# A two-layer hybrid trunk on one core: second MLP operand by quarters, stored products loaded at another product, decays loaded ahead of step sizes

## The chip, the cores and the metric

The kernel runs on one core of a Trainium2 chip. The time is the device time of one execution in microseconds; 2805.24 us is the median of three runs (2802.8 to 2806.19). In the profile, PE is TensorE's matmuls, PEld its weight loads, DVE is VectorE, ACT is ScalarE, POOL is GpSimd and SP is SyncE. POOL and SP mostly issue DMAs here: SP the weights and the mixers' small transfers, POOL most of the activations'.

## The reference, cut to what matters

The input is 1024 prompt tokens and 8 sample tokens of width 1024. Each of two layers is a token mixer and an MLP, both between a modulated norm and a gated residual:

```python
h = rmsnorm(x, norm_mix[l]) * (1.0 + s1) + sh1
out, S, buf = even_mixer(h, ...) if l % 2 == 0 else mamba_mixer(h, ...)
x = x + g1 * out
h = rmsnorm(x, norm_mlp[l]) * (1.0 + s2) + sh2
x = x + g2 * (jnp.square(jax.nn.relu(h @ mlp_w1[l])) @ mlp_w2[l])
```

`mlp_w1` is 1024 x 4096 and `mlp_w2` 4096 x 1024. The odd mixer is a chunked state-space recurrence: a step size `dt` per token and head, its running sum, and the decay `exp` of differences of that sum within a chunk; the sample tokens take one recurrent step of their own. All is float32.

## The kernel before

**Stages.** In the profiled span of 2804.9 us the even mixer takes the first 537 us, its MLP runs to about 1274, the odd mixer to about 2107, the second MLP to the end.

**Precision.** Each float32 operand is split in a high and a low part (ACT copies the high part, DVE subtracts it), and each product is three matmuls, on lines 490 (high x high), 493 and 494. Their operands in a row are `whi`, `wlo` (weights) and `rr`, `hh`, `hl`, `hr`, `x` (activations); `pd` is the accumulator in PSUM.

**The MLP.** Each of its two matrix products is cut 2 x 2, and seven products of sums of the blocks stand for eight. The first half (`AOPS`, loop at line 865) runs over 16 pairs `p` of output rows, with products `q` from 1 to 7. For the pairs in `SPLIT` (the first two and the last four, 12 to 15, among them) products 1 and 2 are done well ahead of the others, and their results go to DRAM: product 1 as `kept` (line 895), the squared ReLU of product 2 as `b` (line 806). They come back when the pair's other products run: `kept(p)` (line 856) loads product 1 into a buffer `t`, and line 886 loads `b` into a slot of `x`. Pair 12 calls for them at its product 6, whose result L899 subtracts from the loaded one. That subtraction is also what frees the product's accumulator, so a later matmul waits for it. POOL issues all of these DMAs, strictly in the order of the code, and a store waits at its head until ACT or DVE has made its data. Ahead of pair 12's product 6 in that queue stand the stores of pair 15's products 1 and 2 and the four loads that `load_op(0, 0)` issues at the end of (15, 2).

**The second half** (loop at line 939) makes products `i` = 0 to 6, each in eight steps `j` of 48 matmuls (the last product in 16 half steps). From `i` = 1 on, steps 0 to 3 take the quarters `q` = 0 to 3 of the operand for one half of the outputs, steps 4 to 7 again for the other. Operand `i` lies in DRAM (`td`) and comes by `load_op(i, kh)` for its halves `kh` = 0 and 1: two tiles `rr`, one for the high parts and one for the low; four loads of two rows of blocks each, issued on POOL; and four chunks of a split, ACT's copy on L843 and DVE's subtraction on L844, that `split_op` hands out at the ends of steps by a table of counts (lines 974 to 977). I call the chunks of the second half chunk 0 to 3: step 2 reads chunks 0 and 1, step 3 chunks 2 and 3. For `i` from 2 to 5 chunk 0 is split at the end of step 7 of the product before, chunks 1 and 2 at the end of step 0, chunk 3 at the end of step 1. A tile's buffers are those of the product before, so loads for a half are issued at step 5 (`kh` = 1 of the next product) and step 7 (`kh` = 0 of the one after).

Between those steps DVE also builds the weights: L451, L453 and L455 add or subtract two weight blocks that SP's loads bring (`t<-W`, `t<-sd`, `raw<-W`), ACT makes the high part on L456, DVE the low part on L457. DVE runs its queue in order, so a chunk of `rr` behind such a sum waits for that sum's DMA too. L964 and L971 apply a finished accumulator to `x`. In the first MLP, steps also hold work on the next layer's modulation (`t<-ada`, L320).

**The odd mixer** works in two halves of the tokens. `odd_dt` makes step sizes, stores the running sums (`csd`), their exponentials (`esd`) and the last column (`cdd`), and for the first half the sample tokens' step sizes (`sd`). A background generator, `rest()`, is stepped along with the other work: it loads `dts` (from `sd`) and `cd`, then transposes on PE. Later `odd_ssd` loads, for each chunk, two broadcast blocks of `csd` (`load(r)`), on which ACT works on L1533. SP's order in this stage is set by a scheduler as it builds the program, not by the code's order alone.

Of the kernel before, what the change touches and what calls it, by code (L numbers as in the profile page):

```python
# [8 lines left out]
F32R = mybir.dt.float32r  # L9
# [5 lines left out]
P = 128  # L15
D = 1024
KT = 8
# [144 lines left out]
def kernel(ctx: ExitStack, tc: tile.TileContext, A: dict):  # L162
# [62 lines left out]
    def dma_aux(out, in_):  # L225

        tc.keep_in_program_order(nc.gpsimd.dma_start(out=out, in_=in_))  # L227
# [557 lines left out]
    def mlp(l, gi, finish, more=None):  # L785
# [44 lines left out]

        R, todo = {}, []

        def load_op(i, kh):

            pool, tag = ((big, M["tags"][0]), (ph.pool, "hr"), (big, M["tags"][1]))[BSET[i][kh]]
            ts = [pool.tile([P, KT * 520], F32R, name="rr", tag=tag, bufs=2) for _ in range(2)]
            hi, lo = R[i, kh] = [t[:, 0:KT * HX].rearrange("p (k t) -> p k t", t=HX) for t in ts]
            d = td[BOPND[BPROD[i]]][kh]

            def parts():  # L840
                for c in range(0, KT, 2):
                    src = lo[:, c:c + 2].bitcast(F32)
                    tc.keep_in_program_order(S.copy(hi[:, c:c + 2], src))  # L843
                    V.tensor_sub(lo[:, c:c + 2], src, hi[:, c:c + 2].bitcast(F32))  # L844
                    yield
            for c in range(0, KT, 2):
                dma_aux(lo[:, c:c + 2].bitcast(F32), d[:, c:c + 2])
            todo.append(parts())

# [15 lines left out]
        for i, (p, q) in enumerate(AOPS):  # L865
            n = APOS[p, q]
            while len(got) <= n // 2:
                got.append(need(f"a{l}", len(got), AHEAD - 1))
            if i == 0:
                bg.drain(hgen.pop(3, None))  # L870
                sg = bg.add(mlp_sums())
                bg.step(sg)
            elif i == 2 * LEAD:
                bg.drain(hgen.pop(2), sg)
                sg = bg.add(mlp_more_sums())
            elif i == 2 * LEAD + 4:
                bg.drain(sg)
            if i == 2 * LEAD - 4:
                kept(0)
                kept(1)  # L880
            if q == 6:
                kept(p)
                if p and p + 1 in keep:
                    kept(p + 1)
            if p in SPLIT and q == (5 if p < 2 else 6):
                dma_aux(slot(p, 1), B[p])
            w = 512 * (n % 2), got[n // 2]
            pt = pd()
            product(w, q, pt)
            pv = pt[:, :, 0:HX // 2]  # L890
            if q == 1:
                U[p, 1] = t2(HX)
                S.copy(v2(U[p, 1]), pv)
                if p in SPLIT:
                    keep[p] = dr.tile([P, HX], F32, name="kept", tag=f"kept{p}")
                    dma_aux(keep[p], U[p, 1])
            elif q == 6:
                U[p, 1], U[p, 2] = saved.pop(p, U[p, 1]), t2(HX)
                V.tensor_sub(v2(U[p, 2]), v2(U[p, 1]), pv)  # L899
            elif q == 7:  # L900
                U[p, 3] = t2(HX)
                V.tensor_add(v2(U[p, 3]), pv, v2(U[p, 2]))
            elif q == 5:
                c = t2(HX)
                V.tensor_add(v2(c), pv, v2(U[p, 3]))
                V.tensor_add(v2(U[p, 2]), pv, v2(U[p, 2]))
                ff_out(p, q, c, -1.0)
            elif q == 2:
                c = t2(HX) if p in SPLIT else U[p, 1]
                V.tensor_add(v2(c), pv, v2(U[p, 1]))  # L910
                ff_out(p, q, c, 1.0)
            elif q == 4:
                c = U[p, 3] if p < NPAIR - 1 else t2(HX)
                V.tensor_add(v2(c), pv, v2(U[p, 3]))
                ff_out(p, q, c, -1.0)
            else:
                V.tensor_add(v2(U[p, 2]), pv, v2(U[p, 2]))
                ff_out(p, q, U[p, 2], 1.0)
            if n % 2:
                prepare(wpos[0] - 1 + AHEAD)  # L920
            if (p, q) == FRONT[1][-1]:
                load_op(0, 0)
            elif p == NPAIR - 2 and q in (7, 5, 4, 3):
                split_op()
            if (p, q) == (NPAIR - 1, 5):
                split_op(4)
                load_op(0, 1)
            bg.tick(2)

        x = new_x()  # L930
        for m in range(KT):
            dma_aux(x[:, m, :], xd[:, m])
        load_op(1, 0)
        acc = tp.tile([P, KT, NS], F32, name="racc", tag="racc", bufs=2)
        V.memset(acc, 0.0)
        fin = finish()
# [2 lines left out]
        for n, (i, hb, q, mp) in enumerate(BOPS):  # L939
            j = n % 8  # L940
            hi, lo = need(f"b{l}", n, AHEAD - 1)
            if n == 8 and more:
                ada[0] = more()
            elif i == 6 and hb == 0 and j == 0:
                ada_steps(99)
            rh, rl = R[i, q // 2]
            seq = BSEQ if i else BFIRST
            qs = [qq for qq, mm in seq if mm == mp]
            for m in (2 * mp, 2 * mp + 1):
                if q == qs[0]:  # L950
                    pts[m] = pd()
                pt = pts[m]
                for b in range(2) if hb is None else (hb,):
                    c = slice(b * hw, b * hw + hw)
                    mm3(pt[:, b, 0:hw], [(hi[:, o:o + P], lo[:, o:o + P], rh[:, k, c], rl[:, k, c])
                                         for k, o in ((q % 2 * 4 + k, 256 * k + m % 2 * P) for k in range(4))],
                        q == qs[0], q == qs[-1])
                if q == qs[-1]:
                    for o, th in BOUT[BPROD[i]]:
                        mt = 4 * o + m  # L960
                        gate = mod[:, gi + mt, 0:1]
                        if hb is None:
                            xv = v2(x[:, mt, th * HX:th * HX + HX])
                            V.scalar_tensor_tensor(xv, pt[:, :, 0:hw], gate, xv, op0=ALU.mult, op1=ALU.add)  # L964
                        else:
                            xv = x[:, mt, th * HX + hb * hw:th * HX + hb * hw + hw]
                            V.scalar_tensor_tensor(xv, pt[:, hb, 0:hw], gate, xv, op0=ALU.mult, op1=ALU.add)
                        if hb != 1:
                            sv = pt[:, 0, 0:4] if th else pt[:, 1, hw - 4:hw]
                            av = acc[:, mt, 4 * th:4 * th + 4]  # L970
                            V.tensor_add(av, sv, av)  # L971
            prepare(wpos[0] - 1 + AHEAD)

            if i == 0:
                split_op((0, 2, 2, 0, 1, 1, 2, 0)[j])
            else:
                split_op((2, 2, 1, 1, 1, 1, 0, 1)[j] if i == 1 else (2, 1, 1, 1, 1, 1, 0, 1)[j] if i < 6 else (2, 1, 0, 0, 0, 0, 0, 0)[j] if hb == 0 else 0)
            if j == (5 if i else 3) and i < 6:
                load_op(i + 1, 1)
            elif j == 7 and i < 5:  # L980
                load_op(i + 2, 0)
# [372 lines left out]
    def dtile(w=136):  # L1354
        t = ph.pool.tile([P, 136], F32, name="dtr", tag="dtr", bufs=4)
        return t[:, :w]

    def odd_dt(hf, o):

        u = need("dt", 0)  # L1360
# [53 lines left out]
            o.dts = ph.pool.tile([P, 2, 16, NS], F32, name="dts")  # L1414

        def rest():
            yield
            if hf == 0:
                for q in range(2):
# [4 lines left out]
            yield  # L1424
            pt = psm()
            PE.transpose(pt[:, 0:P], dtt[:, 0:P], ident)
            PE.transpose(pt[:, P:2 * P], cs[:, 0:P], ident)
            PE.transpose(pt[:, 2 * P:3 * P], dl, ident)
            o.nat = hs3[:, 0:3]
            V.tensor_copy(o.nat.rearrange("p a t -> p (a t)"), pt[:, 0:3 * P])  # L1430
        return bg.add(rest())

    def odd_conv(hf, t, unit, dst):
# [46 lines left out]
    def odd_ssd(hf, g, o):  # L1480
# [6 lines left out]
        St = o.S[g]  # L1487

        def load(r):
            hs = 32 * r + 8 * g  # L1490
            Rs = []
            for q in range(2):
                R = t2(512)
                dma(R, o.csd[hs + 4 * q:hs + 4 * q + 4].rearrange("(o h) t -> o (h t)", o=1).broadcast_to([P, 512]))
                Rs.append(R)
            return Rs

        def load_e(r):
            hs = 32 * r + 8 * g
# [17 lines left out]
            PE.matmul(pc[:, c], Bt[:, c], Ct[:, c], start=True, stop=True)  # L1517
        cb = t3(512)
        V.tensor_mul(a4(cb), a4(pc), cmask.unsqueeze(1).broadcast_to([P, 4, P]))
        Rs = load(0)  # L1520
        yield
        for r in range(4):
            c = slice(r * P, r * P + P)
# [604 lines left out]
```

## Time and profile before

| What | us |
|---|---|
| median of three runs | 2805.24 |
| profiled execution | 2806.7 |
| its span | 2804.9 |
| PE busy | 2654.7 |
| DVE busy | 1983.5 |
| ACT busy | 1485.0 |
| mean granted clock | 0.977 of full speed |

A row of the timeline names the start, the duration, engine, line, operation, output and inputs, and in brackets the idle time ahead of it with what ended that. A row of the waits gives the total, the number of waits and the longest. A row of the windows gives, for one stretch, its length, each engine's busy time with its number of instructions (PE, PEld, DVE, ACT, POOL), the granted clock, the mean busy share of the 16 DMA engines and GB/s.

### The profile page before, as it was taken

The numbers are of one execution on the slowest core, as the hardware profiler recorded it, in microseconds if no ns is written. First come the engines' busy times: TensorE is split into PE (matmuls) and PEld (weight loads), VectorE is DVE, ScalarE is ACT, GpSimd is POOL, SyncE is SP. The second block draws the span as 40 slices with busy tenths as digits, with TensorE's granted clock in tenths as the row PEclk, the third lists the DMA queues.
The fourth block names the chain that finished last, engine by engine and source line by source line (L and its number), as shares of the span: only waits on it lengthen the run. The fifth ranks groups of instructions, "written<-read, shape, count | busy, mean of one in ns | idle before, by whom it ended". The sixth has DMA issues, their size and how long they took to land. (4 is left out here: it accounts for less than half of the span.)

```text
span 2804.9 us, 49250 instructions
## 1 busy us (share of the span) xinstructions
PE 2654.7 (95%) x19442; PEld 2443.9 (87%) x19442; DVE 1983.5 (71%) x3668; ACT 1485.0 (53%) x2409; POOL 266.5 (10%) x492
## 2 busy tenths in 40 slices
PE   6999999999999988998899999999999999999897
PEld 4889888899999977898789897787779999999897
DVE  5666544788757555775789788998778776756676
ACT  5785511464444322356687767878756445433234
POOL 0000000023223100000000000000001322311000
PEclk9999999999999999999899999999999999999998
DMA  8232333257468899834545745444435655779764
GB/s 300 69 107 71 105 121 113 88 191 242 168 204 312 328 334 353 321 129 115 142 148 144 184 122 155 132 132 124 117 105 172 223 184 181 264 284 372 266 214 156
DMA packets 199256, 525.63 MB, mean 187 GB/s; under 512 B 32688, under 2 KB 50736, under 8 KB 199024
## 3 DMA queue, kind: packets, MB, share of 16 engines
q1 hardware_dynamic: 150640, 355.25, 40.3%
q0 software_dynamic: 48384, 167.23, 16.2%
q8 instruction: 153, 2.51, 0.4%
q14 instruction: 79, 0.65, 0.1%
HBM read 408.59 MB, written 113.80 MB: 186 GB/s over the span
## 5 line engine op out<-in xcount | busy, mean ns | idle before, releaser
L490 PE MATMUL pg<-hh,whi 128*128 128x256 f32 (+2 forms) x1616 | 535.8, 332 | 13.5 <-ACT hh L592 6.2
L493 PE MATMUL pd<-rr,whi 128*128 128x258 f32 x1792 | 512.3, 286 | 25.1 <-DVE rr L844 24.9
L493 PE MATMUL pg<-hl,whi 128*128 128x256 f32 (+2 forms) x1616 | 522.8, 324 | 1.9 <-DVE hl L593 1.9
L494 PE MATMUL pg<-hh,wlo 128*128 128x256 f32 (+2 forms) x1616 | 522.0, 323 | 0.0
L490 PE MATMUL pd<-rr,whi 128*128 128x258 f32 x1792 | 513.4, 287 | 0.0
L494 PE MATMUL pd<-rr,wlo 128*128 128x258 f32 x1792 | 510.5, 285 | 1.5 <-DVE wlo L467 1.1
L467 DVE TENSOR_TENSOR wlo<-raw,whi 128x1024 fp32r<-128x1024 f32 x222 | 270.7, 1221 | 216.5 <-ACT whi L466 209.9
L466 ACT CAST whi<-raw 128x1024 fp32r<-128x1024 f32 x222 | 231.4, 1044 | 349.4 <-PE pg L493 192.0
L493 PEld LDWEIGHTS pd<-rr,whi 128*128 128x128 f32 x1792 | 343.6, 192 | 29.2 <-DVE rr L844 27.0
L490 PEld LDWEIGHTS pd<-rr,whi 128*128 128x128 f32 x1792 | 343.7, 192 | 19.0 <-issue 16.5
L490 PEld LDWEIGHTS pg<-hh,whi 128*128 128x128 f32 x1616 | 308.0, 191 | 50.0 <-issue 8.8
L494 PEld LDWEIGHTS pd<-rr,wlo 128*128 128x128 f32 x1792 | 344.0, 192 | 4.0 <-DVE wlo L467 1.8
L493 PEld LDWEIGHTS pg<-hl,whi 128*128 128x128 f32 x1616 | 308.1, 191 | 31.1 <-issue 5.8
L494 PEld LDWEIGHTS pg<-hh,wlo 128*128 128x128 f32 x1616 | 307.4, 190 | 24.4 <-issue 0.7
L490 PE MATMUL pd<-hh,whi 128*128 128x258 f32 x1024 | 293.9, 287 | 18.6 <-DVE t L899 12.6
L493 PE MATMUL pd<-hh,whi 128*128 128x258 f32 x1024 | 292.7, 286 | 0.8 <-DVE hh L695 0.8
L494 PE MATMUL pd<-hh,wlo 128*128 128x258 f32 x1024 | 291.1, 284 | 0.0
L490 PEld LDWEIGHTS pd<-hh,whi 128*128 128x128 f32 x1024 | 196.8, 192 | 21.0 <-issue 13.6
L456 ACT CAST whi<-t 128x1024 fp32r<-128x1024 f32 x64 | 67.0, 1047 | 274.8 <-PE pd L493 116.8
L493 PEld LDWEIGHTS pd<-hh,whi 128*128 128x128 f32 x1024 | 196.3, 192 | 1.9 <-DVE hh L695 1.4
L494 PEld LDWEIGHTS pd<-hh,wlo 128*128 128x128 f32 x1024 | 196.6, 192 | 0.0
L490 PE MATMUL pg<-ffh,whi 128*128 128x264 f32 (+2 forms) x544 | 176.8, 325 | 2.1 <-ACT bcz L1633 1.5
(335 smaller groups left out, 5813.9 us busy)
## 6 DMA issues: line engine op xcount, KB each, us to landing
raw<-W SPq DMA_DIRECT2D x375, 512.0 KB, 4.3
td<-x POOLq DMA_DIRECT2D x224, 258.0 KB, 3.6
rr<-td POOLq DMA_DIRECT2D x112, 516.0 KB, 8.1
t<-ada SPq DMA_DIRECT2D x192, 256.0 KB, 5.4
t<-W SPq DMA_DIRECT2D x32, 512.0 KB, 5.8
sd<-t SPq DMA_DIRECT2D x32, 512.0 KB, 5.8
t<-sd SPq DMA_DIRECT2D x32, 512.0 KB, 5.5
t<-csd SPq DMA_DIRECT2D x64, 256.0 KB, 4.6
```

The costliest lines, as they stand in the source:

```text
L456: S.copy(hi, h)
L466: S.copy(hi, raw)
L467: V.tensor_sub(lo, raw, hi.bitcast(F32))
L490: mm = PE.matmul(pt, wh, xh, start=first and i == 0, stop=False)
L493: PE.matmul(pt, wh, xl, start=False, stop=False)
L494: PE.matmul(pt, wl, xh, start=False, stop=last and i == n - 1)
```

## The change

It has three parts.

1. The second half's operands are loaded by quarters: `load_op(i, q)` makes one tile per quarter that holds high and low parts, with two loads and two chunks of a split. The same loads and chunks are issued as before, the quarters 2 and 0 at step 4 and 6 (of product 0: 2 and 6), the quarters 3 and 1 at step 5 and 7 (3 and 7). The split's tables change: for `i` from 2 to 5 chunks 0 and 1 are split at the end of step 7, chunk 2 at the end of step 0 and chunk 3 at the end of step 1.
2. The loads of `kept` for pairs 12 and 13 and of `b` for pair 12 move from (12, 6) to (15, 1), where they are issued ahead of that product.
3. In the odd mixer, `rest()` first loads the two blocks of `csd` for the first chunk of group 0 (`o.R0`), then makes the transposes, then loads `dts` and `cd`. `odd_ssd` takes them from there for its first chunk.

```diff
-        def load_op(i, kh):
+        def load_op(i, q):
...
-            pool, tag = ((big, M["tags"][0]), (ph.pool, "hr"), (big, M["tags"][1]))[BSET[i][kh]]
-            ts = [pool.tile([P, KT * 520], F32R, name="rr", tag=tag, bufs=2) for _ in range(2)]
-            hi, lo = R[i, kh] = [t[:, 0:KT * HX].rearrange("p (k t) -> p k t", t=HX) for t in ts]
-            d = td[BOPND[BPROD[i]]][kh]
+            pool, tag = ((big, M["tags"][0]), (ph.pool, "hr"), (big, M["tags"][1]))[BSET[i][q // 2]]
+            t = pool.tile([P, KT * 520], F32R, name="rr", tag=tag, bufs=2)
+            hi, lo = R[i, q] = [t[:, j * 4 * HX:(j + 1) * 4 * HX].rearrange("p (k t) -> p k t", t=HX)
+                                for j in range(2)]
+            d = td[BOPND[BPROD[i]]][q // 2][:, q % 2 * 4:q % 2 * 4 + 4]
...
-            if p in SPLIT and q == (5 if p < 2 else 6):
+            if p in SPLIT and q == (5 if p < 2 else 6) and p != NPAIR - TAIL:
                 dma_aux(slot(p, 1), B[p])
+            elif (p, q) == (NPAIR - 1, 1):
+                kept(NPAIR - TAIL)
+                kept(NPAIR - TAIL + 1)
+                dma_aux(slot(NPAIR - TAIL, 1), B[NPAIR - TAIL])
...
-            if i == 0:
-                split_op((0, 2, 2, 0, 1, 1, 2, 0)[j])
-            else:
-                split_op((2, 2, 1, 1, 1, 1, 0, 1)[j] if i == 1 else (2, 1, 1, 1, 1, 1, 0, 1)[j] if i < 6 else (2, 1, 0, 0, 0, 0, 0, 0)[j] if hb == 0 else 0)
-            if j == (5 if i else 3) and i < 6:
-                load_op(i + 1, 1)
-            elif j == 7 and i < 5:
-                load_op(i + 2, 0)
+            split_op(((0, 2, 1, 1, 1, 1, 1, 1), (2, 2, 1, 1, 1, 1, 0, 2), (1, 1, 0, 0, 0, 0, 0, 0))[2 if i == 6 else i][j]
+                     if i in (0, 1, 6) else (1, 1, 1, 1, 1, 1, 0, 2)[j])
+            at = (4, 5, 6, 7) if i else (2, 3, 6, 7)
+            if j in at and i < 6 and i + 1 + at.index(j) // 2 < 7:
+                load_op(i + 1 + at.index(j) // 2, (2, 3, 0, 1)[at.index(j)])
...
         def rest():
+            o.R0 = load_decays(o, 0)
+            yield
...
-        Rs = load(0)
+        Rs = load(0) if g else o.R0
```

What this does to the order of instructions is seen at three places. The first is POOL's queue at the end of the first MLP's first half; `kept<-t` and `b<-t` are the stores of pairs 13 to 15, `t<-kept` the loads for pairs 12 and 13, `x<-b` that of pair 12. Before:

```order
L227 DMA b_8178<-t_8174 128x516
L227 DMA kept<-t_8220 128x516
L227 DMA b_8253<-t_8249 128x516
L227 DMA kept<-t_8286 128x516
L227 DMA b_8319<-t_8315 128x516
L227 DMA rr<-td 128x1032 x4
L227 DMA t_8341<-kept 128x516 x2
L227 DMA x<-b_8112 128x516
```

And now:

```order
L227 DMA b_8178<-t_8174 128x516
L227 DMA kept<-t_8220 128x516
L227 DMA b_8253<-t_8249 128x516
L227 DMA t_8261<-kept 128x516 x2
L227 DMA x<-b_8112 128x516
L227 DMA kept<-t_8290 128x516
L227 DMA b_8323<-t_8319 128x516
L227 DMA rr<-td 128x1032 x4
```

The three loads stand ahead of pair 15's two stores and of the four `rr` loads, where they stood behind all six. The second place is DVE's queue in the second MLP's second half, from the end of the third product's step 7 to the end of the fourth product's step 1. Before, `rr_27172` is that product's second half, chunks 0 to 3:

```order
L457 TENSOR_TENSOR wlo_27293<-t6_27295,whi_27292 128x1024
L844 TENSOR_TENSOR rr_27172<-rr_27172,rr_27171 128x1032
L455 TENSOR_TENSOR t6_27488<-t6_27488,raw_27490 128x1024
L455 TENSOR_TENSOR t6_27561<-t6_27561,raw_27563 128x1024
L457 TENSOR_TENSOR wlo_27362<-t6_27364,whi_27361 128x1024
L844 TENSOR_TENSOR rr_27172<-rr_27172,rr_27171 128x1032 x2
L457 TENSOR_TENSOR wlo_27425<-t6_27427,whi_27424 128x1024
L844 TENSOR_TENSOR rr_27172<-rr_27172,rr_27171 128x1032
```

Now `rr_27110` is the third quarter (chunks 0 and 1) and `rr_27174` the fourth (chunks 2 and 3):

```order
L457 TENSOR_TENSOR wlo_27296<-t6_27298,whi_27295 128x1024
L845 TENSOR_TENSOR rr_27110<-rr_27110 128x1032 x2
L455 TENSOR_TENSOR t6_27488<-t6_27488,raw_27490 128x1024
L455 TENSOR_TENSOR t6_27561<-t6_27561,raw_27563 128x1024
L457 TENSOR_TENSOR wlo_27364<-t6_27366,whi_27363 128x1024
L845 TENSOR_TENSOR rr_27174<-rr_27174 128x1032
L457 TENSOR_TENSOR wlo_27425<-t6_27427,whi_27424 128x1024
L845 TENSOR_TENSOR rr_27174<-rr_27174 128x1032
```

Chunk 1 has passed the two weight sums; chunks 2 and 3 stand where they stood. The third place is SP's queue in the odd mixer's first half. Before:

```order
L221 DMA hs_13009<-cdd 128x128
L221 DMA bcd<-bcz 128x8x1
L221 DMA dts<-sd 64x128 x4
L221 DMA raw<-W 128x1024
L221 DMA t_13620<-csd 128x512
L221 DMA t_13622<-csd 128x512
```

And now:

```order
L221 DMA hs_13009<-cdd 128x128
L221 DMA bcd<-bcz 128x8x1
L221 DMA dts<-sd 64x128 x3
L221 DMA raw<-W 128x1024
L221 DMA dts<-sd 64x128
L221 DMA t_13310<-csd 128x512
L221 DMA t_13312<-csd 128x512
```

The loads of `csd` are still behind all loads of `dts`; one weight load has passed the last of these.

More of the change, by code (lines that the diff above doesn't have):

```diff
@@ L831, in mlp @@
         R, todo = {}, []
-        def load_op(i, kh):
-            pool, tag = ((big, M["tags"][0]), (ph.pool, "hr"), (big, M["tags"][1]))[BSET[i][kh]]
-            ts = [pool.tile([P, KT * 520], F32R, name="rr", tag=tag, bufs=2) for _ in range(2)]
-            hi, lo = R[i, kh] = [t[:, 0:KT * HX].rearrange("p (k t) -> p k t", t=HX) for t in ts]
-            d = td[BOPND[BPROD[i]]][kh]
+        def load_op(i, q):
[4 more added lines that the diff above has]
+            d = td[BOPND[BPROD[i]]][q // 2][:, q % 2 * 4:q % 2 * 4 + 4]
             def parts():
-                for c in range(0, KT, 2):
+                for c in range(0, 4, 2):
                     src = lo[:, c:c + 2].bitcast(F32)
@@ L845, in parts @@
                     yield
-            for c in range(0, KT, 2):
+            for c in range(0, 4, 2):
                 dma_aux(lo[:, c:c + 2].bitcast(F32), d[:, c:c + 2])
@@ L922, in mlp @@
                 load_op(0, 0)
+                load_op(0, 1)
             elif p == NPAIR - 2 and q in (7, 5, 4, 3):
@@ L926, in mlp @@
                 split_op(4)
-                load_op(0, 1)
+                load_op(0, 2)
+                load_op(0, 3)
             bg.tick(2)
@@ L933, in mlp @@
         load_op(1, 0)
+        load_op(1, 1)
         acc = tp.tile([P, KT, NS], F32, name="racc", tag="racc", bufs=2)
@@ L945, in mlp @@
                 ada_steps(99)
-            rh, rl = R[i, q // 2]
+            rh, rl = R[i, q]
             seq = BSEQ if i else BFIRST
@@ L955, in mlp @@
                     mm3(pt[:, b, 0:hw], [(hi[:, o:o + P], lo[:, o:o + P], rh[:, k, c], rl[:, k, c])
-                                         for k, o in ((q % 2 * 4 + k, 256 * k + m % 2 * P) for k in range(4))],
+                                         for k, o in ((k, 256 * k + m % 2 * P) for k in range(4))],
                         q == qs[0], q == qs[-1])
@@ L1356, in dtile, with load_decays @@
         return t[:, :w]
+    def load_decays(o, hs):
+        Rs = []
+        for q in range(2):
+            R = t2(512)
+            dma(R, o.csd[hs + 4 * q:hs + 4 * q + 4].rearrange("(o h) t -> o (h t)", o=1).broadcast_to([P, 512]))
+            Rs.append(R)
+        return Rs
     def odd_dt(hf, o):
@@ L1416, in rest @@
         def rest():
+            o.R0 = load_decays(o, 0)
+            yield
+            yield
+            pt = psm()
+            PE.transpose(pt[:, 0:P], dtt[:, 0:P], ident)
+            PE.transpose(pt[:, P:2 * P], cs[:, 0:P], ident)
+            PE.transpose(pt[:, 2 * P:3 * P], dl, ident)
+            o.nat = hs3[:, 0:3]
+            V.tensor_copy(o.nat.rearrange("p a t -> p (a t)"), pt[:, 0:3 * P])
             yield
@@ L1423, in rest @@
             dma(o.cd, cdd.rearrange("(o p) a -> o (p a)", o=1).broadcast_to([P, P]))
[L1424 to L1430, printed above, removed]
         return bg.add(rest())
@@ L1489, in load @@
         def load(r):
[L1490 to L1496, printed above, removed]
+            return load_decays(o, 32 * r + 8 * g)
         def load_e(r):
```

## The prediction

> **What bounds the kernel now.** I read the first part of the page, then the waits of PE, then the timeline at each of the longest gaps.
>
> ```profile
> span 2804.9 us, 49250 instructions
> PE 2654.7 (95%) x19442; PEld 2443.9 (87%) x19442; DVE 1983.5 (71%) x3668; ACT 1485.0 (53%) x2409; POOL 266.5 (10%) x492
> ...
> PE pd L493 <- DVE rr L844: 24.9, 7, 7.4
> PE pd L490 <- DVE t L899: 12.6, 3, 6.6
> PE psm L1511 <- DVE hs L1430: 2.2, 1, 2.2
> ```
>
> TensorE is busy for 95% of the span, so a gain can only be idle PE time (2804.9 - 2654.7 is at most 150 us) or time at a low clock. The change touches the first two waits: 24.9 us in which the MLPs' last products wait for a chunk of `rr`, and 12.6 us in which a first-half product waits until L899 frees its accumulator. The second, in the second MLP:
>
> ```profile
> 815.36 0.54 POOL L227 DMA_DIRECT2D b<-t  x1 [2.57 <-ACT t L804]
> ...
> 2375.42 0.54 POOL L227 DMA_DIRECT2D b<-t  x1 [2.27 <-ACT t L804]
> 2383.19 0.54 POOL L227 DMA_DIRECT2D b<-t  x1 [5.99 <-ACT t L804]
> 2383.72 2.11 POOL L227 DMA_DIRECT2D rr<-td  x4
> 2387.98 1.08 POOL L227 DMA_DIRECT2D t<-kept  x2 [2.15 <-issue]
> ...
> 2386.94 0.69 DVE L432 TENSOR_TENSOR wlo<-t,whi 128x512 fp32r<-128x512 f32 x1
> 2395.86 0.69 DVE L899 TENSOR_TENSOR t<-t,pd 128x516 f32<-128x516 f32 x1 [8.22 <-DMA t<-kept]
> ...
> 2389.85 0.28 PE L494 MATMUL pd<-x,wlo 128*128 128x258 f32 x1
> 2396.69 0.55 PE L490 MATMUL pd<-hh,whi 128*128 128x258 f32 x1 [6.56 <-DVE t L899]
> ```
>
> The load of `kept` stands in POOL's queue behind a store that waits for ACT and behind four `rr` loads. It is issued at 2387.98 and lands at 2395.8; DVE stands still for 8.22 us, PE for 6.56. The gap also costs clock: the windows show 0.50 for 6.83 us behind it, so 26 matmuls take 4.59 and 5.22 us where 28 take 3.04 at full clock.
>
> ```profile
> core 0: us, PE busy (x) PEld busy (x) DVE busy (x) ACT busy (x) POOL busy (x), PEclk, DMA share, GB/s
> 2393.18:2400.01 6.83, 3.32 (x15) 3.35 (x16) 4.16 (x7) 0.99 (x2) 0.00 (x0) 0.50 0.56 197
> 2396.69:2401.28 4.59, 4.59 (x26) 4.59 (x27) 3.47 (x6) 2.23 (x4) 0.55 (x1) 0.64 0.37 114
> 835.37:840.59 5.22, 5.22 (x26) 5.22 (x27) 3.46 (x6) 2.44 (x4) 0.68 (x2) 0.55 0.39 119
> 840.59:843.63 3.04, 3.04 (x28) 3.04 (x27) 1.44 (x3) 1.27 (x2) 1.50 (x3) 1.00 0.47 183
> ...
> 835.37 0.55 PE L490 MATMUL pd<-hh,whi 128*128 128x258 f32 x1 [5.29 <-DVE t L899]
> ```
>
> **Part 1, the `kept` loads earlier.** Three DMAs (two loads of `kept`, one of `b`) go ahead of the last pair's two stores, on POOL: behind the store of 2375.42, so issued by about 2377.6 at 0.54 us each. Taking the 7.8 us that the load took here, it lands at 2385.4. In the first MLP the store ahead stands at 815.36, which gives a landing at 825.4, 4.7 us before PE stops (835.37 - 5.29 = 830.08). The L899 step then runs straight behind L432, at 2387.6, and ends at 2388.3, before PE comes to the accumulator at 2390.13. So the wait goes whole and its slow clock with it. First MLP: 5.29 + (5.22 - 3.04) = 7.5 us. Second: 6.56 + (4.59 - 3.04) = 8.1 us. **Sum: -15.6.** The two stores come 1.6 us later; nothing reads them for tens of us. Next to be late is L401's weight load:
>
> ```profile
> 2380.26 0.69 DVE L401 TENSOR_TENSOR t<-raw 128x512 f32<-128x512 f32 x1 [5.40 <-DMA raw<-W]
> 2386.90:2389.95 3.05, 3.05 (x27) 3.02 (x26) 0.69 (x1) 0.01 (x1) 1.60 (x3) 1.00 0.98 355
> ```
>
> The Trainium skill's page "DMA: Bandwidth & Descriptors", section "Issuing engines are not separate DMA queues", says that transfers of every issuing engine run on the same 16 DMA engines, which speaks against moving loads into this wait. By that rule and the 355 GB/s above, three transfers of 258 KB push the weight load back by up to 2.2 us, and the L899 step ends at 2390.5 instead of 2388.3: at most 0.4 us of the 8.1 would be lost. No run so far shows it, and the sum leaves it out.
>
> **Part 2, `rr` by quarters.** No DMA, copy or subtraction is added (rows of L844 stay at 1.22 us each); chunks 0 to 3 of a half are now two quarters, and chunk 1 is split a step earlier, next to chunk 0. PE needs chunk 1 in step 2 of a product and chunk 3 in step 3, one step later: 48 matmuls, 5.7 us by the undisturbed stretch below (47.00 us for 395). Chunk 3 keeps its place on DVE, behind the weight sums. The fourth product of the second MLP:
>
> ```profile
> 2487.00:2534.00 47.00, 47.00 (x395) 47.00 (x395) 33.10 (x43) 16.51 (x17) 4.19 (x8) 1.00 0.62 209
> ...
> 2601.03 1.23 DVE L455 TENSOR_TENSOR t<-t,raw 128x1024 f32<-128x1024 f32 x1 [1.24 <-DMA t<-sd]
> 2603.30 2.37 DVE L844 TENSOR_TENSOR rr<-rr 128x1032 fp32r<-128x1032 f32 x2
> 2606.73 1.23 DVE L844 TENSOR_TENSOR rr<-rr 128x1032 fp32r<-128x1032 f32 x1
> ...
> 2604.58 0.58 PE L493 MATMUL pd<-rr,whi 128*128 128x258 f32 x1 [7.11 <-DVE rr L844]
> 2601.39:2608.22 6.83, 3.64 (x17) 3.64 (x18) 6.56 (x6) 0.00 (x0) 0.00 (x0) 0.50 0.95 320
> ```
>
> PE waits 7.11 us for chunk 1, resumes at 2604.58, loses (2608.22 - 2604.58)/2 = 1.8 to the clock and reaches chunk 3 at 2604.58 + 5.7 + 1.8 = 2612.1. Afterwards chunk 1 is early, PE reaches chunk 3 at 2597.47 + 5.7 = 2603.2 and finds it done at 2606.73 + 1.23 - 1.15 (one subtraction fewer ahead; the pair of 2603.30 takes 2.37, one 1.22) = 2606.8: a wait of 3.6 us and a slow stretch of about 1.8 behind it. Gain 5.3 - 1.8 = **3.5**. The other sites in the same way:
>
> ```profile
> 1005.31 0.58 PE L493 MATMUL pd<-rr,whi 128*128 128x258 f32 x1 [7.40 <-DVE rr L844]
> 1008.80 1.23 DVE L844 TENSOR_TENSOR rr<-rr 128x1032 fp32r<-128x1032 f32 x1
> 1000.54:1010.78 10.24, 5.47 (x25) 5.47 (x26) 8.62 (x10) 2.00 (x2) 0.00 (x0) 0.50 0.93 349
> 1187.85 0.58 PE L493 MATMUL pd<-rr,whi 128*128 128x258 f32 x1 [5.03 <-DVE rr L844]
> 1184.86:1191.69 6.83, 3.85 (x18) 3.85 (x19) 6.35 (x6) 0.00 (x0) 0.00 (x0) 0.50 0.50 154
> 1193.31 1.23 DVE L453 TENSOR_TENSOR t<-raw,t 128x1024 f32<-128x1024 f32 x1 [2.10 <-issue]
> 2550.71 0.39 PE L493 MATMUL pd<-rr,whi 128*128 128x258 f32 x1 [2.06 <-DVE rr L844]
> 2548.65:2556.72 8.07, 6.01 (x50) 6.01 (x51) 7.70 (x7) 2.72 (x3) 0.00 (x0) 1.00 1.02 397
> 1736.00:1743.00 7.00, 6.11 (x25) 5.10 (x26) 7.00 (x32) 6.94 (x14) 0.00 (x0) 0.76 0.21 77
> 2654.30 0.39 PE L493 MATMUL pd<-rr,whi 128*128 128x258 f32 x1 [1.86 <-DVE rr L844]
> 2661.46 0.39 PE L493 MATMUL pd<-rr,whi 128*128 128x258 f32 x1 [1.16 <-DVE rr L844]
> ```
>
> - First MLP, third product: today chunk 3 is reached at 1005.31 + 5.7 + 2.7 (half of 1010.78 - 1005.31) = 1013.7; it will be ready at 1008.9. Less 1.8 for the clock, -3.0. DMA share is 0.93 there, so a third I expect to come back as later `t<-ada` waits: **-2**.
> - First MLP, sixth product: the weight sum of 1193.31 now stands ahead of chunk 3, which becomes ready three operations later, 1193.31 + 3 x 1.2 = 1196.9; today PE passes there at 1187.85 + 5.7 + 1.9 = 1195.5, the clock's share included. With 1.4 later and 1.8 of clock behind the new wait: **+3**.
> - Second MLP, third product: chunk 3 is in time, **-2**. Fifth: chunk 3 ended the wait of 2661.46 and is ready no sooner; PE comes to it at 2654.30 - 1.86 + 5.7 = 2658.1, the two waits merge into one of 3.3 us, and its clock is added: **+1.8**. Sixth and seventh, gaps below 1 us: **-1.5** together.
>
> Sum with the 3.5 above: **-4.2**. Bounds: all 24.9 us vanish with their 6.5 of slow clock (1.9 + 1.8 + 2.7), -31.4; or all five products with a gap above 1.8 us go as the sixth of the first MLP does, 5 x 3 = +15.
>
> The slow clock in these terms rests on the rows: after gaps of 5.0 to 7.4 us it is 0.50; after the gap of 2.06 us it stayed at 1.00, and behind the 2.2 us wait at L1511 (which ended at 1736) it was 0.76; so 3.3 us should cost some, and 1.8 is taken from its nearest rows, the gaps of 5.0 and 7.1. The Trainium skill's page "TensorE: Matmul & The Clock Gate", section "Part 1: The HAM clock gate (the "warmup" mystery)", puts the threshold at an idle window of about 3.4 us; by that rule the merged wait of 3.3 us would cost no clock, and the sum would be 1.8 lower; the row of 1736 speaks against it.
>
> **Part 3, the decays.** In the built order the loads of `csd` in the first half still follow all four `dts` loads, and PE's, DVE's and ACT's rows keep their order; one `raw<-W` moves ahead of the last `dts`. So this wait stays:
>
> ```profile
> 1319.63 0.40 ACT L1533 ACTIVATE t<-t,hs 128x128 f32<-128x128 f32 x1 [8.63 <-DMA t<-csd]
> ```
>
> In the second half `csd` passes one `st_ss` load that is then up to 4 us later. I take **0**, between -2 and +2.
>
> **Sum:** 2806.7 (the profiled execution; span 2804.9) - 15.6 - 4.2 = 2786.9. The median of the runs, 2805.24, is 1.5 below the profiled execution, so **2785**.
>
> **Rivals.**
> 1. All waits for `rr` go (chance 0.15): quarters' waits find chunk 3 done, because DMAs issued one step earlier pull the weight sums forward. For: DVE is 71% busy. Against: chunk 3's place. 2805.2 - 15.6 - 31.4 = 2758.
> 2. The waits only move from chunk 1 to chunk 3 (0.24): part 2 is 0, give or take 2; 2805.2 - 15.6 = 2790. For: the sixth product above.
> 3. The first MLP takes its gain back (0.10): DMA, at 0.93 of its time in the windows above, is the bound there and does not shift with PE. Its 7.5 and 2 are lost of 19.8 in all: 2795.
> 4. Slower (0.06): the even quarters' loads, one step earlier, push ahead of weight loads. Each moved quarter is 1032 KB, at 349 GB/s 3.0 us. Some ten fall where the DMA share above is 0.93 to 1.02; from seven on that put their 3.0 us on DVE's weight sums the 19.8 are gone. With all ten: 2805.2 - 19.8 + 30 = 2815.
> 5. Part 1 doesn't do what it says, because a buffer still in use holds the early loads back on POOL (0.03): part 2 alone, 2801.
>
> **Numbers.** The forecast has the remaining 0.42. The range runs from 2768, half of the way to rival 1's bound, to 2798: rivals 2 and 3, and half of the +15. Outside lie most of rival 1 (0.11), rivals 4 and 5 (0.09). 0.2%, 5.6 us, is about what a measurement of this kernel can tell from no change: the forecast and rivals 1 and 2 lie under 2799.6, most of 3 too (0.86 in all), rival 5 and the rest of 3 within it (0.08), rival 4 above (0.06).
>
> **What would show it.** The row of the wait for L899 (in the new line numbers) gone and no gap by 830 and 2390, clock 1.00 there: part 1. `rr` waits of 15 to 20 us, each about one step later than now: part 2; near zero, rival 1; as large as now, rival 2. PE waiting more for `t<-ada`: rival 3. L451 to L455 waiting longer for DMA: rival 4. The forecast is wrong if the stretch from 977 to 1165 does not start earlier by the first MLP's 7.5 us.

## The result and the profile after

The changed kernel takes 2783.69 us (median of four runs, 2782.93 to 2789.04) against 2805.72 for the kernel before beside it: a ratio of 0.9927, 95% interval 0.991 to 0.9944, so 20.5 us less, between 15.7 and 25.3. Now and then an execution comes out far slower, and the ratios here and below leave these out: one of e1_kept_alone (4994 us) and one of e3_decays_alone (10436 us). The profiled execution is the slowest of its runs, 2789.04 us with a span of 2787.3.

The head and the first part of the page:

```profile
span 2787.3 us, 49297 instructions
PE 2654.0 (95%) x19442; PEld 2445.2 (88%) x19442; DVE 1983.6 (71%) x3668; ACT 1484.8 (53%) x2409; POOL 267.2 (10%) x492
```

The waits of PE (who waits, for whom, us in all, times, the longest), for the rows that were shown of before; L904 is the old L899, L845 the old L844:

```profile
PE pd L320 <- DMA t<-ada: 16.2, 9, 3.3
PE pd L493 <- DVE rr L845: 11.8, 6, 3.8
PE pd L494 <- DVE wlo L457: 3.3, 1, 3.3
PE pd L494 <- DVE wlo L467: 3.0, 2, 2.6
PE psm L1521 <- DVE hs L1439: 2.2, 1, 2.2
```

The rows of before that the prediction does not show:

```profile
PE pd L320 <- DMA t<-ada: 11.2, 3, 4.9
PE pd L494 <- DVE wlo L467: 1.1, 1, 1.1
PE pd L494 <- DVE wlo L457: 0.3, 1, 0.3
```

PE is as busy as before to 0.7 us, so what went in all is idle time; slow clock that went at one place came back at others. No row for L904 is left among the waits. The waits for `rr` are halved, 11.8 us where there were 24.9, and the longest is 3.8 where it was 7.4. Against this, `t<-ada` stands at 16.2 us, and low parts of weights (`wlo`) at 3.3 and 3.0. One profile does not size such a row: the changed kernel's second profile (e5_change_again, below) has 16.4 for `rr` and 9.5 for `t<-ada`.

The timeline of POOL and then of DVE at the end of the second MLP's first half (start, us, engine, line, operation, the idle time ahead of it and what ended it):

```profile
2368.63 0.54 POOL L227 DMA_DIRECT2D b<-t  x1 [1.70 <-ACT t L804]
2369.16 1.08 POOL L227 DMA_DIRECT2D t<-kept  x2
2370.35 0.54 POOL L227 DMA_DIRECT2D x<-b  x1
2370.88 0.55 POOL L227 DMA_DIRECT2D kept<-t  x1
2376.57 0.55 POOL L227 DMA_DIRECT2D b<-t  x1 [5.14 <-ACT t L804]
2377.11 0.54 POOL L227 DMA_DIRECT2D rr<-td  x1
...
2377.26 0.69 DVE L432 TENSOR_TENSOR wlo<-t,whi 128x512 fp32r<-128x512 f32 x1
2377.86 0.69 DVE L904 TENSOR_TENSOR t<-t,pd 128x516 f32<-128x516 f32 x1
```

The loads are issued 7.4 us ahead of the store that they used to stand behind. DVE's subtraction starts at the end of L432, with no idle time ahead of it. Counted by matmuls, PE comes to the two places of the old gaps at 834.2 and 2383.1. The windows around them (busy time of PE, PEld, DVE, ACT, POOL, then the granted clock, the DMA share and GB/s) show PE without idle time and the clock whole:

```profile
830.00:836.00 6.00, 6.00 (x52) 6.00 (x52) 3.70 (x7) 3.16 (x6) 0.55 (x1) 1.00 0.99 374
2380.00:2390.00 10.00, 10.00 (x85) 10.00 (x85) 6.87 (x12) 4.86 (x8) 4.64 (x9) 1.00 0.97 364
```

PE's timeline at the longest waits left for `rr` and for low parts, in the first MLP's sixth product (step 3) and in the second MLP's fourth (step 2) and fifth (step 1):

```profile
1185.27 0.39 PE L493 MATMUL pd<-rr,whi 128*128 128x258 f32 x1 [3.77 <-DVE rr L845]
2582.19 0.48 PE L493 MATMUL pd<-rr,whi 128*128 128x258 f32 x1 [3.24 <-DVE rr L845]
2627.73 0.58 PE L494 MATMUL pd<-rr,wlo 128*128 128x258 f32 x1 [3.27 <-DVE wlo L457]
```

And the window at the second of them, where the wait of 3.24 us ends at 2582.19:

```profile
2570.00:2590.00 20.00, 16.76 (x127) 16.55 (x126) 15.54 (x20) 4.67 (x6) 0.00 (x0) 0.91 0.87 315
```

PE is idle for 3.24 us of these 20, and the granted clock is 0.91: it is 0.50 from 2582.32 to 2585.73 and 1.00 in the rest.

### The profile page after: what moved, and what is told of

Read it like the earlier page. It is cut to its first block, busy times and chain, and to the rows that moved or that the text cites. A ratio compares the mean times of both kernels' runs of the same rounds, so it can differ in the third digit from the quotient of the medians.

```text
span 2787.3 us, 49297 instructions
## 1 busy us (share of the span) xinstructions
PE 2654.0 (95%) x19442; PEld 2445.2 (88%) x19442; DVE 1983.6 (71%) x3668; ACT 1484.8 (53%) x2409; POOL 267.2 (10%) x492
## 3 DMA queue, kind: packets, MB, share of 16 engines
q1 hardware_dynamic: 150640, 355.25, 40.8%
## 5 line engine op out<-in xcount | busy, mean ns | idle before, releaser
L493 PE MATMUL pd<-rr,whi 128*128 128x258 f32 x1792 | 514.2, 287 | 11.8 <-DVE rr L845 11.8
```

The source lines that it names most:

```text
L493: PE.matmul(pt, wh, xl, start=False, stop=False)
```

## The experiments

All times are set against runs of the kernel before on the same chip. On the chips of these runs that kernel had medians of 2816.5 to 2821.3 us, some 12 us above the first chip's, and scattered by about 8 us to both sides; so ratios are compared. The intervals reach 4 to 7 us to each side, and a difference of less than about 5 us between two kernels is not told apart. "Less" is the ratio's share of the kernel before's median. The last column is from the one profiled execution of each run: the time from the first matmul that reads `rr` to the last, in both MLPs together. It holds the stages that part 2 changes and leaves out the scatter of the others; in the kernel before it is 739.9 us, in the changed kernel 738.5, and 734.6 in a second profile of that (e5_change_again).

| Run | Ratio, 95% interval | us less | second halves, us |
|---|---|---|---|
| e1_kept_alone | 0.9956, 0.994 to 0.9971 | 12.4 | 747.6 |
| e2_quarters_alone | 0.9966, 0.9952 to 0.9981 | 9.6 | 738.0 |
| e3_decays_alone | 1.0002, 0.9987 to 1.0016 | -0.6 | 740.9 |
| e4_kept_after_store | 0.9932, 0.9917 to 0.9948 | 19.2 | 750.4 |
| e5_change_again | 0.9936, 0.9914 to 0.9959 | 18.0 | 734.6 |
| e6_late_chunks_early | 0.9877, 0.986 to 0.9894 | 34.6 | 718.5 |
| e7_loads_at_old_steps | 0.9922, 0.9908 to 0.9937 | 22.0 | 739.4 |
| e8_order_of_splits_only | 0.9919, 0.9904 to 0.9934 | 22.8 | 738.7 |
| e9_decays_pinned | 0.9911, 0.9896 to 0.9927 | 25.1 | 733.4 |
| e10_late_chunks_and_pin | 0.9872, 0.9855 to 0.989 | 36.1 | 728.2 |
| e11_late_chunks_no_kept | 0.9927, 0.9904 to 0.995 | 20.6 | 727.2 |
| e12_halves_all_early | 0.9885, 0.9859 to 0.9911 | 32.4 | 730.9 |

### The three parts alone

The kernel before with the early loads:

```diff
-            if p in SPLIT and q == (5 if p < 2 else 6):
+            if p in SPLIT and q == (5 if p < 2 else 6) and p != NPAIR - TAIL:
                 dma_aux(slot(p, 1), B[p])
+            elif (p, q) == (NPAIR - 1, 1):
+                kept(NPAIR - TAIL)
+                kept(NPAIR - TAIL + 1)
+                dma_aux(slot(NPAIR - TAIL, 1), B[NPAIR - TAIL])
```

> The kernel before with only the early loads of kept and b for pair 12 (part 1). Theory: the waits for the subtraction of the loaded product go with their slow clock, 7.5 us in the first MLP and 8.1 in the second, so 15.6 us faster than before, 2789 to 2791 us, no PE gap at the first halves' ends, and the rr waits as before (some 25 us). Rival, the first MLP's second half is bound by DMA and takes its 7.5 back: 8 us faster, 2797 to 2798, with the waits for t<-ada or rr longer by some 7 us in the first MLP.

The kernel before with the change's `load_op(i, q)`, its split tables and its steps of loading, and nothing else:

```diff
-        def load_op(i, kh):
+        def load_op(i, q):
...
-            elif j == 7 and i < 5:
-                load_op(i + 2, 0)
+            at = (4, 5, 6, 7) if i else (2, 3, 6, 7)
+            if j in at and i < 6 and i + 1 + at.index(j) // 2 < 7:
+                load_op(i + 1 + at.index(j) // 2, (2, 3, 0, 1)[at.index(j)])
```

> The kernel before with only the operands by quarters (part 2). Theory: about 4 us faster, 2800 to 2803 us, with rr waits at about half and new waits for t<-ada and weights in their place. Rival, all that is saved at rr comes back at t<-ada and wlo: within 2 us of before, 2804 to 2807. Second rival, part 2 carries more than was reckoned: over 7 us faster, under 2798.

The kernel before with the odd mixer's part:

```diff
         def rest():
+            o.R0 = load_decays(o, 0)
...
-        Rs = load(0)
+        Rs = load(0) if g else o.R0
```

> The kernel before with only the odd mixer's part (part 3). Theory: 0, give or take 2 us (2803 to 2808 us), ACT's wait for csd of 8 to 9 us and the PE gap of about 5 us behind it still there. Rival: the odd mixer's 3 us that the changed kernel's profile gained came from this part, 2801 to 2803 us.

The early loads give 12.4 us (8.2 to 16.9), the quarters 9.6 (5.4 to 13.5), the decays nothing. The parts add up to 21.4, and the whole change measured 20.5 and 18.0. For the first, 15.6 lies within the interval; for the second, 4.2 lies just outside and the second rival's "over 7" holds the 9.6. How much of the 9.6 is scatter stays open, since the second halves of this run are only 2.9 us shorter than with the decays alone (738.0 against 740.9). Waits of PE, for the early loads alone and then for the decays alone, which stand for the kernel before on this chip:

```profile
PE pd L493 <- DVE rr L844: 31.7, 9, 8.2
PE pd L490 <- DVE t L903: 1.5, 1, 1.5
```

```profile
PE pd L493 <- DVE rr L844: 26.7, 10, 7.3
PE pd L490 <- DVE t L899: 12.9, 2, 7.4
PE pg L490 <- ACT xy L1458: 5.1, 1, 5.1
```

With the early loads alone the 12.9 us at L899 fall to 1.5 (a wait at 2276.7, away from the two sites), and the waits for `rr` rise by 5.0. The second halves are 6.7 us longer than with the decays alone, and 9.5 longer in e4_kept_after_store, which has the old order of splits too; all of that lies in the second MLP (348.1 us, then 356.6 and 358.7). So some of the gain comes back there. The last row is the odd mixer's gap, unchanged.

### What delayed the loads of `kept`

The three loads put ahead of the four `rr` loads only (the condition at the old place as in e1_kept_alone):

```diff
             if (p, q) == FRONT[1][-1]:
+                kept(NPAIR - TAIL)
+                kept(NPAIR - TAIL + 1)
+                dma_aux(slot(NPAIR - TAIL, 1), B[NPAIR - TAIL])
                 load_op(0, 0)
```

> The kernel before with the three loads placed ahead of the four rr loads only, behind pair 15's second store, which waits for ACT. Theory (the place in POOL's queue sets when the loads land): issued some 2.1 to 4.3 us sooner than before, landing about 2 us too late; a gap of about 2 us stays in each MLP, without or with little slow clock, 9 to 12 us faster than before, 2793 to 2797. Rival (the rr loads ahead of them were the whole delay, by their bandwidth): no gap, 15 us faster as with the full move, 2789 to 2791.

The theory's numbers failed: 19.2 us less (14.7 to 23.4), and no gap, as the rival had it. The timeline of POOL and of DVE at the end of the second MLP's first half:

```profile
2384.62 0.54 POOL L227 DMA_DIRECT2D b<-t  x1 [5.47 <-ACT t L804]
2385.15 1.07 POOL L227 DMA_DIRECT2D t<-kept  x2
2386.22 0.54 POOL L227 DMA_DIRECT2D x<-b  x1
2386.74 0.54 POOL L227 DMA_DIRECT2D rr<-td  x1
...
2389.25 0.69 DVE L899 TENSOR_TENSOR t<-t,pd 128x516 f32<-128x516 f32 x1 [2.48 <-PE pd L494]
```

The loads are still behind the store that waits 5.47 us for ACT, yet DVE now waits for PE's product and no longer for the load. What changed is that the `rr` loads come behind. In the rows of before that the prediction shows, `kept` follows 4.3 us after the first of them (2387.98 against 2383.72). The view of `kept`'s tile at this place says how long its loads took to land, here and then with the decays alone:

```profile
DMA to landing us min/median/max: 4.0/4.1/4.2
```

```profile
DMA to landing us min/median/max: 7.8/7.9/7.9
```

So the four `rr` loads, 2 MB, were the decisive part: 4.3 us of queue and some 3.7 of transfer. The changed kernel shows that the transfer also depends on what else is under way. Its `kept` loads stand ahead of `rr` too, but took 6.6 and 6.7 us:

```profile
DMA to landing us min/median/max: 6.6/6.6/6.7
```

Their windows say why this may be. First the changed kernel, then this one:

```profile
2368.00:2370.00 2.00, 2.00 (x19) 2.00 (x18) 0.14 (x1) 0.93 (x2) 1.37 (x3) 1.00 1.03 346
```

```profile
2384.00:2386.00 2.00, 2.00 (x19) 2.00 (x18) 1.31 (x3) 0.84 (x2) 1.38 (x3) 1.00 0.15 56
```

At their issue the DMA engines are full in the one (share 1.03) and nearly idle in the other (0.15). In the changed kernel the second load lands at 2369.7 + 6.7 = 2376.4, some 1.5 us ahead of the subtraction at 2377.86, so it costs nothing. That this kernel is better than the full move, as the ratios have it, is not shown: their intervals overlap, and neither has a gap of PE at this place.

### What the quarters bring

First the changed kernel once more, for comparison on this chip:

> The changed kernel again, as the measure for the next three on one chip. It should be about 20 us faster than before (0.8%), since the parts alone gave 12, 10 and 0.

It was 18.0 us under before (11.5 to 24.2). Its six executions lie between 2784.6 and 2806.4 us, and the profiled one is the fastest of them. Its waits:

```profile
PE pd L493 <- DVE rr L845: 16.4, 7, 4.3
PE pd L320 <- DMA t<-ada: 9.5, 6, 3.8
```

Then chunks 2 and 3 split by the end of step 7, ahead of the weight sums:

```diff
-            split_op(((0, 2, 1, 1, 1, 1, 1, 1), (2, 2, 1, 1, 1, 1, 0, 2), (1, 1, 0, 0, 0, 0, 0, 0))[2 if i == 6 else i][j]
-                     if i in (0, 1, 6) else (1, 1, 1, 1, 1, 1, 0, 2)[j])
+            split_op(((0, 2, 1, 1, 1, 1, 1, 1), (2, 2, 1, 1, 1, 1, 1, 3), (0, 0, 0, 0, 0, 0, 0, 0))[2 if i == 6 else i][j]
+                     if i in (0, 1, 6) else (0, 0, 1, 1, 1, 1, 1, 3)[j])
```

> The changed kernel with chunks 2 and 3 split at the end of step 7 of the product before, ahead of the weight sums that they stood behind (tables alone: one chunk at step 6, three at step 7). Theory (what is left of the rr waits, some 12 us and slow clock, comes from the place behind the sums): the rr waits fall under 5 us and the time by 4 to 8 us against the changed kernel. Rival (DVE is late because of its weights, so it is their low parts that PE then waits for): rr waits fall, but waits for wlo of L457 take their place and the time stays within 3 us. Second rival: the four chunks in a row at step 7 delay the end of the product (L972), and it is slower by 3 or more.

34.6 us under before, so 16.6 under the change as run beside it, more than the 4 to 8 expected. Two other pairs below differ by the same edit: with the pinned loads it gives 36.1 - 25.1 = 11.0 us (e10 against e9), with operands by halves, on two chips, 32.4 - 22.8 = 9.6 (e12 against e8). So it is worth some 10 to 17 us. The waits of PE, and then the window that was shown of the changed kernel:

```profile
PE pd L320 <- DMA t<-ada: 11.1, 6, 3.5
PE pd L494 <- DVE wlo L457: 2.9, 3, 1.5
PE pd L493 <- DVE rr L845: 0.9, 2, 0.6
```

```profile
2570.00:2590.00 20.00, 20.00 (x169) 20.00 (x168) 14.62 (x19) 7.69 (x8) 1.06 (x2) 1.00 1.00 386
```

The waits for `rr` are down to 0.9 us, and low parts (L457: 2.9 us) did not take their place. The place of the chunks behind the weight sums was the cause of what was left. The wait at 2582.19 had cost more than its idle time: where the changed kernel has clock 0.91 between 2570 and 2590 us, this one has 1.00 and no idle PE. That the waits as a whole cost more than their rows is not shown: 15.5 us of `rr` waits fewer (16.4 to 0.9) go with second halves that are 16.1 us shorter here (734.6 to 718.5), but in the other two pairs 11.9 and 19.6 us fewer go with 5.2 and 7.8. The spans of the two profiled executions are only 1.7 us apart (2782.8 and 2781.1), since other stages, which the edit leaves as they are, were slower in the second.

The quarters' loads at the steps of before:

```diff
-            at = (4, 5, 6, 7) if i else (2, 3, 6, 7)
-            if j in at and i < 6 and i + 1 + at.index(j) // 2 < 7:
-                load_op(i + 1 + at.index(j) // 2, (2, 3, 0, 1)[at.index(j)])
+            if j == (5 if i else 3) and i < 6:
+                load_op(i + 1, 2)
+                load_op(i + 1, 3)
+            elif j == 7 and i < 5:
+                load_op(i + 2, 0)
+                load_op(i + 2, 1)
```

> The changed kernel with the quarters' loads issued at the steps of before (5 and 7, two quarters at a time); split order unchanged. Theory (the order of the splits did it, not the time of the loads): within 3 us of the changed kernel, t<-ada and rr waits about the same. Rival (loads one step earlier crowd out t<-ada): t<-ada waits on pd fall from 16 to about 11 and it is 3 to 5 us faster. Second rival (early loads are the gain): 4 or more slower, with rr waits of 20 us.

The early `kept` loads and the new order of splits, with operands by halves as before (of the diff, the split's table alone):

```diff
-                split_op((2, 2, 1, 1, 1, 1, 0, 1)[j] if i == 1 else (2, 1, 1, 1, 1, 1, 0, 1)[j] if i < 6 else (2, 1, 0, 0, 0, 0, 0, 0)[j] if hb == 0 else 0)
+                split_op((2, 2, 1, 1, 1, 1, 0, 2)[j] if i == 1 else (1, 1, 1, 1, 1, 1, 0, 2)[j] if i < 6 else (1, 1, 0, 0, 0, 0, 0, 0)[j] if hb == 0 else 0)
```

> Operands by halves as before, loads as before, but with the changed kernel's order of splits (chunks 0 and 1 at step 7, chunk 2 at step 0, chunk 3 at step 1), and with the early loads of kept. Theory (moving one chunk past the sums is the whole gain): within 3 us of the changed kernel. Rival (quarters are needed, since a half's chunks come too late for step 7): slower than the changed kernel by 4 or more, with rr waits at the size of before.

The two are 22.0 and 22.8 us under before, not to be told from the change's 18.0 and 20.5. `t<-ada` on `pd` was 14.1 and 10.9 us, `rr` 11.9 and 19.6. Neither the quarter tiles nor the earlier loads are seen in the time: as far as these intervals tell, the order of the splits is what part 2 brings.

Last, halves with the early loads of `kept` and all late chunks early (of the diff, the split's table alone):

```diff
+                split_op((2, 2, 1, 1, 1, 1, 1, 3)[j] if i == 1 else (0, 0, 1, 1, 1, 1, 1, 3)[j] if i < 6 else 0)
```

> Operands by halves, with loads and layout of before, the early loads of kept, and all four late chunks split by the end of step 7 (one at step 6, three at step 7). Theory (only the order of the splits counts, not the quarters): as with quarters, 1.2% under before, rr waits under 3 us. Rival (the half's last loads, issued at step 5, land too late for a split at step 7, and DVE stands still on them): 1.0% under before or less, with DVE waits for the rr loads.

32.4 us under before (25.1 to 39.8), as with quarters. No wait of PE for `rr` is left in its profile, and DVE has none for the `rr` loads; low parts of L457 cost 8.4 us and the end of a product (`racc`, L975) 7.2, so here other waits take part of their place.

### The decays, and both together

The first half's `csd` loads held ahead of `dts`; the flag makes the scheduler keep the order of the code:

```diff
+            pin, pinned_sp[0] = pinned_sp[0], hf == 0
             o.R0 = load_decays(o, 0)
+            pinned_sp[0] = pin
...
+                pinned_sp[0] = True
                 for q in range(2):
...
+            pinned_sp[0] = pin
             dma(o.cd, cdd.rearrange("(o p) a -> o (p a)", o=1).broadcast_to([P, P]))
```

> The changed kernel with the first half's csd loads held ahead of the four dts loads in SP's queue as built. Theory (part 3 gave nothing because the scheduler left csd behind dts): ACT's wait of 8 to 9 us for csd near 1310 falls under 3, the PE gap of 5 us there goes with its slow clock, and the kernel is 5 to 7 us faster than the changed one (about 1.0% under before). Rival (the dts loads that come later now hold DVE, which stands in front of the weights): DVE waits for dts until some 1320, a PE gap of 3 us or more stays, and the time is within 2 us of the changed kernel's.

The timeline of SP, ACT and PE, in the changed kernel and then in this one:

```profile
1301.24 1.81 SPq L221 DMA_DIRECT2D dts<-sd  x3
1303.11 0.58 SPq L221 DMA_DIRECT2D raw<-W  x1
1303.73 0.45 SPq L221 DMA_DIRECT2D dts<-sd  x1
1304.22 1.86 SPq L221 DMA_DIRECT2D t<-csd  x2
...
1317.07 0.40 ACT L1543 ACTIVATE t<-t,hs 128x128 f32<-128x128 f32 x1 [8.82 <-DMA t<-csd]
1319.20 0.45 PE L490 MATMUL pg<-hh,whi 128*128 128x264 f32 x1 [5.11 <-ACT xy L1463]
```

```profile
1299.34 0.90 SPq L221 DMA_DIRECT2D t<-csd  x2
1302.29 0.33 SPq L221 DMA_DIRECT2D raw<-W  x1
1302.66 8.23 SPq L221 DMA_DIRECT2D dts<-sd  x4
...
1312.85 0.40 ACT L1547 ACTIVATE t<-t,hs 128x128 f32<-128x128 f32 x1 [7.46 <-DMA t<-csd]
1314.98 0.39 PE L490 MATMUL pg<-hh,whi 128*128 128x264 f32 x1 [3.75 <-ACT xy L1467]
```

The theory fell. `csd` is ahead of `dts` now, but from its issue to ACT's start there pass 13.5 us, where there passed 12.9 behind `dts`; ACT's wait falls by 1.4 us, PE's by 1.4, and DVE's wait for `dts` rises from 5.4 to 10.2 us. The rival's two signs, a gap of over 3 us and the longer wait for `dts`, are there. The time, 25.1 us under before (20.6 to 29.3), is not told from the change's. Why `csd` takes 13 us here, where all its loads have a median of 4.6 on the page of after, is narrowed by a window of this run:

```profile
1302.00:1304.00 2.00, 2.00 (x19) 2.00 (x18) 2.00 (x6) 1.99 (x4) 0.00 (x0) 1.00 0.93 34
```

The DMA engines are busy for 0.93 of these 2 us and yet move only 34 GB/s, and so in the next 2, and the two weight loads (`raw<-W`) issued beside `csd` take 13.0 us in the median, where the page of after has 4.9. So the DMA engines at that time, rather than the place in SP's queue, seem to make `csd` late; what slows them is not shown.

Both edits together, the late chunks and the pinned loads:

> Both: chunks 2 and 3 split by the end of step 7, and csd held ahead of dts. Theory: the two add up, 5 to 7 us under the kernel with the late chunks early (1.23% under before), so 1.4% under before, about 2777 us where before takes 2817. Rival as for the pinned loads alone: 1.2 to 1.3% under before.

36.1 us under before (31.0 to 40.8), 1.5 from e6_late_chunks_early and not told apart from it: the rival again. The intervals of these two lie wholly under both of the change's; that of the halves with all chunks early (0.9859 to 0.9911) touches the first of them (0.991 to 0.9944).

The changed kernel with late chunks early, but part 1 undone (the diff of e1_kept_alone, backwards):

> Late chunks early, with the loads of kept and b for pair 12 where they stood before. Theory (with hardly any rr wait left, nothing takes back what the early loads of kept save): 15 us slower than the same kernel with them, 0.7% under before. Rival (the 12 us measured alone are all that they are worth): 12 us slower or less, 0.8% or more under before.

20.6 us under before, so the early loads are worth 34.6 - 20.6 = 14.0 us there; in its profile the wait for the subtraction is back with 11.0 us. That lies between theory and rival, and the intervals don't part the two.

## Why the prediction was right, and where it was not

**Time.** 2785 was forecast and 2783.69 measured, a gain of 20.5 by the ratio where the sum had 19.8. That it is so close is luck in part: alone, part 1 measured 3.2 us less than its term and part 2 5.4 more, and the two errors nearly cancel.

**Where the time went.** The profiles before and after have the same 19442 matmuls, so that the start of each can be compared. Across the first old gap the changed kernel gets 7.6 us ahead, across the second 8.3, where 7.5 and 8.1 were forecast. From the first matmul on `rr` to the last it takes 1.2 us more in the first MLP (forecast +1) and 2.6 less in the second (forecast -5.2). So part 1 is right to a few tenths at its two places, and the second halves, where part 2 acts, gain 1.4 in this pair where 4.2 was forecast.

**Part 1** (-15.6) went as written: issue ahead of the two stores, the subtraction straight behind L432, no gap, clock 1.00. Alone it measured 12.4, where the second MLP's second half took some back, which no term had, and 14.0 (e6 against e11) where hardly any `rr` waits were left. The reason was one step off: I took a landing time of 7.8 us for granted at any place in the queue. It is 4.0 and 4.2 us where the DMA engines are nearly idle, 6.6 to 6.7 where they are full, and 7.8 to 7.9 behind the `rr` loads, so part of the old wait was transfer time, not only POOL's queue. The 0.4 us that was worked out from the Trainium skill's "DMA: Bandwidth & Descriptors", section "Issuing engines are not separate DMA queues", did not show: PE has no gap there.

**Part 2** (-4.2): alone it measured 9.6, with 4.2 just outside the interval, but the second halves of the changed kernel are only 1.4 and 5.3 us shorter than before (738.5 and 734.6 against 739.9). Against the early loads alone (747.6), which lose time there, they are 9.1 and 13.0 shorter. So the term was too small by the runs' times, and by how much is not settled. Right was the mechanism: a wait goes from chunk 1 and in part comes back behind weight sums, and the order of splits is all that is seen in the time. Wrong were sizes and places. The first MLP's sixth product was put at +3, because the sum of 1193.31 was taken to keep its time; the load of one of its two blocks waits for a buffer that a low part (L457) now frees earlier (the load was issued at 1186.67, now at 1176.46), the sum runs at 1181.71, and PE's wait there was 3.77 us at 1185.27, not the 8.4 that the term stands for. In the second MLP the fourth product still waits in step 2 (3.24 us), since chunks 0 and 1 too are behind the sums that precede step 7's end, the last of which waited 4.46 us for a DMA; the term has nearly this wait (3.6 us), but for chunk 3 in step 3, so that its size fits is luck. The fifth waits in step 1 for a low part (3.27 us), and the first MLP's second product has a new wait for a chunk in step 1 (0.75 and 1.07 us, by 935); no term had these.

**The signs.** Those of part 1 came. The `rr` waits are 11.8 us in one profile and 16.4 in the other, where 15 to 20 were named, and of the three long ones two came in step 3, as forecast (the first MLP's sixth product and the second's fifth, 2.84 us where 3.3 was forecast), while the second MLP's fourth stayed in step 2. The stretch from 977 does not start 7.5 us earlier: the matmul that stood there starts 0.9 us earlier, or 5.0 if the 4.1 us are set aside by which this execution was behind ahead of the first old gap. Up to 935 it was 7.5; the new wait of the second product took 2.4. At 1165 it is 11.2 by the same count.

**Part 3** (0) was right: alone 1.0002, and the queue as built still had `csd` behind `dts`.

**Rivals.** That all `rr` waits go did not come true here. The run with late chunks early gets there (0.9 us of waits), though in another way than the rival had it: the chunks pass the weight sums, the loads do not pull the sums forward. The price was lower than 31.4 us: with the loads of `kept` where they stood, it is 20.6 under before (e11_late_chunks_no_kept, 1.1 us of `rr` waits left). The hand-back to `t<-ada` is seen in one profile of the changed kernel (16.2 us) and not in the other (9.5), so it isn't shown to be the change's; the first MLP kept its gain in this pair, 7.6 us ahead behind the gap and 6.5 at its end. Crowding by earlier loads is not seen: L451 to L455 wait 101.9 us for DMA where they waited 106.8 before, and with the loads at the old steps the time is the same within the intervals.

**The rule on the clock.** The Trainium skill, in "TensorE: Matmul & The Clock Gate", section "Part 1: The HAM clock gate (the "warmup" mystery)", asks for an idle window of about 3.4 us before the clock falls. The trace agrees in one place and not in another. The merged wait of the fifth product, to which the prediction gave 1.8 us of slow clock against this rule, came as 2.84 us, and behind it, from 2645.51 to 2652.34, the clock is 1.00. But behind the wait of 3.24 us that ends at 2582.19 there are 3.41 us at half clock. So the 1.8 us was one of two outcomes (more rows are in the last section).

## What to carry to other kernels

Where an in-order engine both prepares weights that wait for DMA and splits an operand that has long landed, put the split ahead of the first instruction that can wait; the size of the tiles and the time of the loads showed nothing in the time here. A small load that a subtraction waits for belongs ahead of large loads in the same queue, since here it waited for their transfer and not only for their issue. And look at the built order before reckoning with a moved load: the scheduler had undone the third part.

## What the runs showed of the hardware

A load of 258 KB took 4.0 to 4.2 us to land with the DMA engines at a share of 0.15 as it was issued, 6.6 to 6.7 us at 1.03, and 7.8 to 7.9 us behind four loads of 516 KB in its queue.

Whether a PE gap below 3.4 us costs clock is not told by its length. In the profile after, two waits of 3.27 us end at 1037.75 and at 2627.73; the windows start there:

```profile
1037.75:1044.58 6.83, 6.83 (x56) 5.99 (x56) 0.19 (x1) 0.00 (x0) 0.00 (x0) 1.00 1.03 406
2627.73:2633.52 5.79, 5.79 (x27) 5.79 (x28) 5.79 (x14) 0.00 (x0) 0.00 (x0) 0.50 0.48 175
```

The first cost nothing, the second ran at half clock. A wait of 2.1 us in the odd mixer is followed by full clock in the profile after (from 1628.21) and by 3.41 us at half clock in e6_late_chunks_early (from 1627.56). Half clock lasted 3.41, 6.83 or 10.24 us at a time (from 2582.32, 2626.69 and 1247.71 in the profile after). So a wait costs its idle time, and 1.7 us or more of clock only where such a stretch stands behind it.
